# The fourth column pair of the first quarter of both up projections by seven block products instead of eight, with its vector-engine work ordered behind the split of the second half of x

## The chip, the cores and the metric

The kernel runs on one core of a Trainium2 chip. The metric is device time in microseconds (us), lower is better: 1263.74 us is the median of three runs before the change (1261.43 to 1265.73). A core has a matrix engine (TensorE, PE in the profile), a vector engine (VectorE, DVE), a scalar engine (ScalarE, ACT), a general engine (GpSimd, POOL), a queue that here only issues transfers (SyncE, SP), and 16 DMA engines. Each engine runs its instructions in the order in which the program lists them; across engines they wait for each other by semaphores.

## The reference

The program is a trunk of two layers over 512 frames of 1024 features, in float32. Layer 0 mixes by a gated linear recurrence, layer 1 by differential attention over a shared key and value projection. Each layer ends with the same MLP, and each part has a norm before it and one after it. What the change touches is the first product of both MLPs:

```python
D_MODEL = 1024; SEQ = 512; D_FF = 4 * D_MODEL

def squared_relu_mlp(h, w_up, w_down):
    u = jax.nn.relu(h @ w_up)
    return (u * u) @ w_down

# in reference(), per layer
ff = squared_relu_mlp(rms_norm(h, mlp_norm_pre[layer]), mlp_w_up[layer], mlp_w_down[layer])
h = h + rms_norm(ff, mlp_norm_post[layer])
```

`w_up` is 1024 x 4096 and `w_down` 4096 x 1024. The kernel keeps activations transposed: features lie on the 128 partitions, frames along the free axis.

## The kernel before

**Split numbers.** TensorE multiplies a reduced float32 (`fp32r` in the profile). To keep the precision of float32, each operand is split in two, `hi` (a rounded copy, written by ACT) and `lo` (the rest, `value - hi`, written by DVE), and every product is three matmuls (`mm3`, line 114 in the profile through the wrapper `pe.matmul`): hi x hi, hi x lo, lo x hi. Weights come from memory into a `raw` tile (four buffers of 128 x 1024 numbers), ACT writes `whi` from it and DVE writes `wlo` (eight buffers each; `split_w`, lines 172 and 173, `split_b`, lines 200 and 201).

**The MLP.** `block` runs it in four quarters `q` of the 4096 inner columns. In each quarter the up projection makes 1024 inner columns, which are squared and split into `uhi` and `ulo` (`split_u` and `keep_u`, lines 469 to 475), and then the down projection (`dn`) adds their product to `zacc`. An up quarter is four pairs of 256 columns. In quarter 0 all four pairs are computed directly: for each half of the 512 frames and each 128 columns, eight row blocks `kt` of x, three matmuls each, every one 256 frames wide. In quarters 1 to 3 (`up_pairs`, class `Pair`) each pair is a 2 x 2 block product by Strassen's scheme in Winograd's form, with seven products instead of eight: the row blocks of x by even and odd `kt` and by half of the frames make four blocks, and so do the weights. A product is four row blocks of three matmuls, 12 in all. For this a pair needs four weight tiles: "a" (two blocks as they are), "d" (the fourth block; one load for two pairs), "s" and "t" (sums of blocks). The sums of "s" begin in the transfer: SP loads one block twice into the raw tile (line 518) and POOL issues a transfer that adds two others to it (line 519). Those of "t" are made by DVE in the raw tile of "a" (lines 527, 528) before it is split a second time.

**The sums of x.** `sums_x` makes four sums of the blocks of x in place in `zacc` (lines 486 and 488) and splits them: three into tiles `t` of their own (491, 492), the fourth into the place of x's even row blocks of the second half (496, 497), when the direct products have read it. Before the change this stands behind the direct products of quarter 0, and quarter 1 is its first user.

**The order of the work.** PE runs in the order of the program text as `Plan` interleaves it: the main chain (projections) and side chains such as `bounds` (the norms), which are given time by a written estimate of each matmul's cost; `until(("x", name, h))` lets the direct products of half `h` begin when the chain has listed the splits of x's half `h`. The order of ACT, DVE, POOL and SP is made by the framework's scheduler from priorities and its own estimates of when things are ready; side chains have a higher priority. `tc.issue_after(ins)` orders the instructions of its block that stand on the engine of `ins` behind `ins`; it does nothing to other engines. `bounds` for x's second half starts with the last columns of the projection before: sums of squares, a sum over the partitions on PE (`ps_mr`), `rsqrt_rows` (lines 289 to 303, ACT and DVE), then for each of four row block pairs the scaling, the sum with the residual, and x's split: `xhi` on ACT (389), `xlo` on DVE (390), and the store of the residual by POOL (391). The variable `marks` is a dictionary in which instructions are kept for such orderings.

## Time and profile before

| | us |
|---|---|
| median of three runs | 1263.74 |
| lowest and highest | 1261.43, 1265.73 |
| the profiled execution, its own time | 1259.98 |
| its span (first to last instruction) | 1258.1 |
| PE busy in the span | 1234.5 |
| DVE, ACT, POOL busy | 828.9, 669.9, 96.0 |
| mean granted TensorE clock | 0.997 |

Times in profile lines are microseconds from the start of the span. A line of the timeline has the start, the duration, the engine, the line of the kernel, the operation, output and inputs with their shapes and, in brackets, how long the engine had been idle before and what it waited for. A busy PE is not a PE at its peak, since matmuls overlap: the distance between the starts of two matmuls is what counts. Names of tiles stand without their numbers, so `whi_a` is the rounded copy of any "a" tile.

### The profile page before, as it was taken

The page shows a single profiled execution, that of the slowest core. Times are in us where ns is not written, and L with a number is a line of the kernel's source. Part 1 is how long each engine was busy: PE and PEld are TensorE (multiplying, and loading weights), DVE is VectorE, ACT ScalarE, POOL GpSimd, SP SyncE. Part 2 cuts the span into 40 slices and gives each one's busy share as a digit, 9 for nine tenths or more (in the row PEclk, how much of TensorE's full clock was granted, in tenths as well). Part 3 has the DMA queues.
Part 4 walks back from the last instruction along what each step waited for, and adds up shares of the span by engine and source line. Part 5 has one row for each costly group of instructions (what it writes and reads, how often), then busy time and mean ns, then how long its engine had stood idle before and what let it go on. Part 6 is the DMA issues. An engine that isn't in the chain of part 4 may idle for free.

```text
span 1258.1 us, 21436 instructions
## 1 busy us (share of the span) xinstructions
PE 1234.5 (98%) x8440; PEld 1119.2 (89%) x8440; DVE 828.9 (66%) x1649; ACT 669.9 (53%) x1244; POOL 96.0 (8%) x174
## 2 busy tenths in 40 slices
PE   9999999999999999999999999999999999999996
PEld 7889899999988989989999788889998898988996
DVE  6878887867854735636498978564785473663645
ACT  6454545437742724616456877664773371561732
POOL 0202211110000000000100000001000000000000
PEclk9999999999999999999999999999999999999998
DMA  7224544244366564635526322222435365463522
GB/s 255 90 51 116 112 109 122 88 152 137 105 160 130 169 142 109 182 86 145 191 78 192 115 88 84 85 81 88 152 111 150 93 180 120 114 188 77 162 98 67
DMA packets 56726, 156.44 MB, mean 124 GB/s; under 512 B 6289, under 2 KB 8594, under 8 KB 56626
## 3 DMA queue, kind: packets, MB, share of 16 engines
q1 hardware_dynamic: 45920, 120.34, 30.4%
q0 software_dynamic: 10464, 34.61, 13.0%
q8 instruction: 66, 1.08, 0.3%
q14 instruction: 34, 0.28, 0.1%
q10 hardware_dynamic: 242, 0.13, 0.0%
HBM read 145.35 MB, written 9.70 MB: 123 GB/s over the span
## 4 chain that ended last, share of the span: by engine, by line
PE 87%; DVE 5%; ACT 3%; DMA 3%; issue 2%; POOL 0%; SPq 0%; DVEq 0%; ACTq 0%
PE dn L114 21%; PE ux L114 9%; PE up L114 7%; PE qf L114 7%; PE kq L114 6%; PE dn_h L114 5%; PE uz L114 4%; PE bo_h L114 3%; PE ao_h L114 3%; PE gl L114 3%; PE v L114 2%; PE g L114 2%; PE uy L114 2%; PE i L114 2%; PE lg L114 2%
## 5 line engine op out<-in xcount | busy, mean ns | idle before, releaser
L114 PE MATMUL dn<-uhi,whi_dn 128*128 128x512 f32 x384 | 152.0, 396 | 0.0
L114 PE MATMUL dn<-uhi,wlo_dn 128*128 128x512 f32 x384 | 151.9, 396 | 0.0
L114 PE MATMUL dn<-ulo,whi_dn 128*128 128x512 f32 x384 | 151.8, 395 | 0.0
L114 PEld LDWEIGHTS dn<-uhi,whi_dn 128*128 128x128 f32 x384 | 72.2, 188 | 17.8 <-ACT r L570 0.7
L200 ACT ACTIVATE whi_a<-raw_a 128x1024 fp32r<-128x1024 f32 x24 | 25.4, 1058 | 117.5 <-PE dn L114 114.0
L114 PEld LDWEIGHTS dn<-uhi,wlo_dn 128*128 128x128 f32 x384 | 72.2, 188 | 17.4
L114 PEld LDWEIGHTS dn<-ulo,whi_dn 128*128 128x128 f32 x384 | 72.2, 188 | 16.8
L173 DVE TENSOR_TENSOR wlo_dn<-raw_dn,whi_dn 128x1024 fp32r<-128x1024 f32 x64 | 76.6, 1220 | 5.9 <-ACT whi_dn L172 4.6
L475 DVE TENSOR_TENSOR ulo<-r,uhi 128x1024 fp32r<-128x1024 f32 (+1 forms) x40 | 40.2, 1010 | 53.9 <-ACT uhi L474 53.9
L114 PE MATMUL up<-xhi,wlo_up 128*128 128x256 f32 x256 | 72.1, 281 | 1.0 <-DVE wlo_up L173 1.0
L114 PE MATMUL up<-xhi,whi_up 128*128 128x256 f32 x256 | 72.6, 284 | 0.0
L114 PE MATMUL up<-xlo,whi_up 128*128 128x256 f32 x256 | 71.8, 281 | 0.0
L172 ACT ACTIVATE whi_dn<-raw_dn 128x1024 fp32r<-128x1024 f32 x64 | 65.7, 1051 | 7.2 <-PE up L114 3.0
L114 PE MATMUL dn_h<-uhi,whi_dn 128*128 128x256 f32 x240 | 66.6, 278 | 0.0
L114 PE MATMUL dn_h<-uhi,wlo_dn 128*128 128x256 f32 x240 | 66.3, 276 | 0.0
L114 PE MATMUL dn_h<-ulo,whi_dn 128*128 128x256 f32 x240 | 66.3, 276 | 0.0
L617 DVE TENSOR_TENSOR zacc<-dn,zacc 128x512 f32<-128x512 f32 x32 | 22.1, 691 | 59.1 <-PE dn L114 59.0
L519 POOL DMA_DIRECT2D raw_s<-in_w_us_dram x24 | 20.8, 866 | 488.8 <-DMA raw_s<-in_w_us_dram 301.6
L114 PE MATMUL qf<-xhi,whi_qf 128*128 128x512 f32 x128 | 52.7, 411 | 1.2 <-ACT xhi L686 0.6
L200 ACT ACTIVATE whi_t<-raw_a 128x1024 fp32r<-128x1024 f32 x24 | 25.5, 1061 | 49.4 <-PE dn L114 27.2
L114 PE MATMUL qf<-xlo,whi_qf 128*128 128x512 f32 x128 | 50.7, 396 | 0.3 <-DVE xlo L687 0.3
L114 PE MATMUL qf<-xhi,wlo_qf 128*128 128x512 f32 x128 | 50.7, 396 | 0.0
(533 smaller groups left out, 4124.5 us busy)
## 6 DMA issues: line engine op xcount, KB each, us to landing
raw_dn<-in_w_dn_dram SPq DMA_DIRECT2D x64, 512.0 KB, 4.3
raw_a<-in_w_us_dram SPq DMA_DIRECT2D x24, 512.0 KB, 4.3
raw_s<-in_w_us_dram SPq DMA_DIRECT2D x48, 256.0 KB, 4.3
raw_s<-in_w_us_dram POOLq DMA_DIRECT2D x24, 512.0 KB, 6.4
raw_up<-in_w_up_dram SPq DMA_DIRECT2D x16, 512.0 KB, 4.1
raw_wkv<-in_w_kv_dram SPq DMA_DIRECT2D x16, 512.0 KB, 3.7
raw_qf<-in_w_qf_dram SPq DMA_DIRECT2D x14, 512.0 KB, 4.7
raw_d<-in_w_us_dram SPq DMA_DIRECT2D x12, 512.0 KB, 4.4
```

The costliest lines, as they stand in the source:

```text
L114: nc.tensor.matmul(out, lhsT, rhs, **kw)
L172: last_split[:] = [a.activation(hi, raw, AF.Copy)]
L173: v.tensor_tensor(lo, raw, hi.bitcast(F32), op=ALU.subtract)
L200: a.activation(hi, raw, AF.Copy)
L475: v.tensor_tensor(ulo[pr][:, :, lo:hi], r, uhi[pr][:, :, lo:hi].bitcast(F32), op=ALU.subtract)
L519: g.dma_start(rs, ws[p, :, 0:2, :], accum_op=ALU.add)
L617: v.tensor_tensor(z, pss[n4], z, op=ALU.add)
```

## The change

In quarter 0 of both MLPs the first three pairs stay direct. The fourth is computed as a `Pair`, so `sums_x` is now used in quarter 0. The weights are laid out anew for this: `w_up` holds the first 512 columns (four raw tiles) and `w_up2` the next 256 (two raw tiles of four row blocks each); `w_us` holds thirteen pairs in a row in place of three quarters of four. The pair of quarter 0 has a "d" tile of half the size for itself, the later pairs share theirs by twos as before. While this pair's weights are fetched and split, the DVE instructions are ordered behind the last subtraction of x's split (`marks["x"]`, the one of the second half by then).

```diff
@@ -387,7 +387,7 @@
             x = r if gpre is None else t
             a.activation(xhs[pr], x, AF.Copy)
-            v.tensor_tensor(xls[pr], x, xhs[pr].bitcast(F32), op=ALU.subtract)
+            marks["x"] = v.tensor_tensor(xls[pr], x, xhs[pr].bitcast(F32), op=ALU.subtract)
             g.dma_start(res[h][:, 2 * pr:2 * pr + 2, :], r)
...
             def __init__(self, q, p, ts):
-                self.p, self.nm, ws = p, f"{layer}_{q}_{p}", w_us[layer, q - 1]
+                self.p, self.nm = p, f"{layer}_{q}_{p}"
+                n = 4 * q + p - 3
+                ws = w_us[layer, n]
                 self.t1, self.t3, self.t2, self.t4 = ts
...
                 ra = raw("a")
-                nc.sync.dma_start(ra, ws[p, :, 0:3:2, :])
+                nc.sync.dma_start(ra, ws[:, 0:3:2, :])
 
                 rs = raw("s")
                 for i in range(2):
-                    nc.sync.dma_start(rs[:, i, :], ws[p, :, 3, :])
-                g.dma_start(rs, ws[p, :, 0:2, :], accum_op=ALU.add)
-                if p % 2 == 0:
+                    nc.sync.dma_start(rs[:, i, :], ws[:, 3, :])
+                g.dma_start(rs, ws[:, 0:2, :], accum_op=ALU.add)
+                if q == 0:
+                    rd = wp.tile([P, 1, 512], F32, tag="raw", name=f"raw_d{self.nm}", bufs=4)
+                    nc.sync.dma_start(rd, ws[:, 1:2, :])
+                    a22s[:] = split_b(rd, f"d{self.nm}") * 2
+                elif p % 2 == 0:
                     rd = raw("d")
-                    nc.sync.dma_start(rd, ws[p:p + 2, :, 1, :].rearrange("a p f -> p a f"))
+                    nc.sync.dma_start(rd, w_us[layer, n:n + 2, :, 1, :].rearrange("a p f -> p a f"))
                     a22s[:] = split_b(rd, f"d{self.nm}")
...
-        def up_pairs(q, ts):
-
-            one = Pair(q, 0, ts)
+        def up_pairs(q, ts, first=0, after=None):
+
+            with tc.issue_after(after.ins) if after is not None else nullcontext():
+                one = Pair(q, first, ts)
             yield from one.begin()
-            for p in range(1, 5):
+            for p in range(first + 1, 5):
                 yield from one.go_on(p == 4)
                 if p < 4:
                     other = Pair(q, p, ts)
                     yield from other.begin()
                 yield from one.end()
-                one = other
+                if p < 4:
+                    one = other
 
         for q in range(4):
             if q == 0:
-                wt = [load_w(w_up[layer, i], 512, None, f"up{layer}_{i}") for i in range(2)]
+                wt = [load_w(w_up[layer], 512, None, f"up{layer}_0"), load_w(w_up2[layer], 256, None, f"up{layer}_1")]
                 for h, (lo, hi) in enumerate(halves):
                     yield until(("x", name, h))
-                    for pr in range(4):
+                    for pr in range(3):
                         ps = mmt(f"up{layer}_{h}_{pr}").rearrange("p (j t) -> p j t", j=2)
                         for j in range(2):
-                            n = 2 * pr + j
                             for kt in range(8):
-                                wmm(ps[:, j, :], wt[n // 4], kt, (n % 4) * P, xhi, xlo, lo, hi, kt == 0, kt == 7)
+                                wmm(ps[:, j, :], wt[pr // 2], kt, (pr % 2 * 2 + j) * P, xhi, xlo, lo, hi, kt == 0, kt == 7)
                                 yield 0
                         split_u(ps, pr, lo, hi, f"r{layer}_{h}_{pr}")
                 ts = sums_x()
+                yield from up_pairs(q, ts, 3, marks["x"])
             else:
                 yield from up_pairs(q, ts)
```

## The prediction

> **What bounds the kernel now.** I began with the page's first part.

> ```profile
> span 1258.1 us, 21436 instructions
> ...
> PE 1234.5 (98%) x8440; PEld 1119.2 (89%) x8440; DVE 828.9 (66%) x1649; ACT 669.9 (53%) x1244; POOL 96.0 (8%) x174
> ```

> TensorE (PE) is busy 98% of the span, so every matmul taken out shortens the end, unless PE then waits for something that had time to spare. The question is therefore local: how many PE microseconds go, and which of the inputs of the new pair, and of what stands before it, come too late. Next I read where up's first quarter lies in PE's timeline (layer 0; layer 1 runs the same code) and what four pairs by seven products take in the second quarter.

> ```profile
> 304.81 0.28 PE L114 MATMUL up<-xhi,whi_up 128*128 128x256 f32 x1
> ...
> 305.15 0.28 PE L114 MATMUL up<-xhi,whi_up 128*128 128x256 f32 x1
> ...
> 307.77 0.39 PE L114 MATMUL up<-xhi,wlo_up 128*128 128x256 f32 x1 [0.50 <-DVE wlo_up L173]
> ...
> 309.70 1.03 PE L114 MATMUL ps_mr<-ss_ao,onesd 128*128 128x256 f32 x4
> 310.38 0.47 PE L114 MATMUL up<-xhi,whi_up 128*128 128x256 f32 x1
> ...
> 327.52 0.60 PE L114 MATMUL ps_mr<-ss_ao,onesd 128*128 128x256 f32 x2
> 327.77 0.47 PE L114 MATMUL up<-xhi,whi_up 128*128 128x256 f32 x1
> ...
> 351.98 0.39 PE L114 MATMUL dn<-uhi,whi_dn 128*128 128x512 f32 x1
> 352.21 0.39 PE L114 MATMUL dn<-ulo,whi_dn 128*128 128x512 f32 x1
> ...
> 398.45 0.28 PE L114 MATMUL ux<-xhi,whi_a 128*128 128x256 f32 x1
> ...
> 438.62 0.39 PE L114 MATMUL dn<-uhi,whi_dn 128*128 128x512 f32 x1
> ```

> The direct quarter runs from 304.81 to 351.98: 47.17 us for 384 matmuls. Out of that come the wait of 0.50 and the two sums that cut in (309.70 to 310.38 is 0.68, 327.52 to 327.77 is 0.25): 45.74 us, or 0.119 per matmul. There is hardly a wait in it, so PE sets the time here.

> The third view is ACT and DVE around the start of that quarter, because they make x's second half.

> ```profile
> 308.24 1.06 ACT L172 ACTIVATE whi_up<-raw_up 128x1024 fp32r<-128x1024 f32 x1
> 310.92 1.06 ACT L172 ACTIVATE whi_up<-raw_up 128x1024 fp32r<-128x1024 f32 x1 [1.61 <-DMA raw_up<-in_w_up_dram]
> 312.33 1.06 ACT L172 ACTIVATE whi_up<-raw_up 128x1024 fp32r<-128x1024 f32 x1 [0.35 <-DMA raw_up<-in_w_up_dram]
> 313.29 0.46 ACT L289 ACTIVATE ss_ao<-ps_mr,epsc 128x256 f32<-128x256 f32 x1
> 313.78 0.42 ACT L297 ACTIVATE ss_ao<-ss_ao 128x256 f32<-128x256 f32 x1
> ```

> ```profile
> 306.49 1.22 DVE L173 TENSOR_TENSOR wlo_up<-raw_up,whi_up 128x1024 fp32r<-128x1024 f32 x1
> ...
> 307.96 1.22 DVE L173 TENSOR_TENSOR wlo_up<-raw_up,whi_up 128x1024 fp32r<-128x1024 f32 x1
> ...
> 314.56 0.42 DVE L299 SCALAR_TENSOR_TENSOR ss_ao<-ps_mr,ss_ao 128x256 f32<-128x256 f32 x1
> ...
> 325.73 0.68 DVE L390 TENSOR_TENSOR xlo<-zacc,xhi 128x512 fp32r<-128x512 f32 x1
> 326.33 0.42 DVE L341 TENSOR_TENSOR ss_ao<-ss_ao 128x256 f32<-128x256 f32 x1
> 326.67 2.48 DVE L486 TENSOR_TENSOR zacc<-zacc 128x1024 f32<-128x1024 f32 x2
> ...
> 337.19 0.69 DVE L475 TENSOR_TENSOR ulo<-r,uhi 128x512 fp32r<-128x512 f32 x1 [0.56 <-ACT uhi L474]
> ...
> 348.49 0.69 DVE L475 TENSOR_TENSOR ulo<-r,uhi 128x512 fp32r<-128x512 f32 x1 [3.52 <-ACT uhi L474]
> ```

> The reader is to see a queue that holds up the x chain. The sum that L289 reads is done at 309.70 + 1.03 = 310.73, yet L289 starts at 313.29, because two weight copies whose transfers land late stand before it on ACT. From L299 on the chain is dense; the last split of x's second half (L390) ends at 325.73 + 0.68 = 326.41. PE wants that half after 192 matmuls, at 304.81 + 192 x 0.119 + 0.50 + 0.68 + 0.25 = 329.1. So the late copies cost nothing today: x is 2.7 us early.

> **The change part by part.**

> *Removed on PE.* A pair computed directly is 96 matmuls, 96 x 0.119 = 11.43 us. By seven products it is 84. The four pairs of the second quarter took 438.62 - 398.45 = 40.17, or 10.04 each; the waits in them were

> ```profile
> PE ux L114 <- DVE r L565: 0.5, 1, 0.5
> ```

> so 9.92 without. The gain is 1.39 to 1.51 per MLP; I take 1.45, so 2.9 us for both. The floor is 12 matmuls at the spacing by which the quarter starts (304.81 to 305.15 for three, 0.113), 1.36. [...]

> *Moved: the need for x's second half.* The first half now has 144 matmuls and ends at 304.81 + 144 x 0.119 + 0.50 + 0.68 = 323.1. Its last two of eight row blocks of x are wanted 18 matmuls into the second half, at 323.1 + 2.1 = 325.2. If the chain stayed where it is, PE would wait 326.4 - 325.2 = 1.2 us. But the two late copies of up weights go: six up tiles are left, the last copied at 308.24. What takes their place on ACT is the pair's own copies (a and d), which the new ordering on the x split doesn't hold, since that split and the queueing are DVE's. The transfers take, from issue to landing (last column, us):

> ```profile
> raw_s<-in_w_us_dram SPq DMA_DIRECT2D x48, 256.0 KB, 4.3
> raw_s<-in_w_us_dram POOLq DMA_DIRECT2D x24, 512.0 KB, 6.4
> ```

> There are four raw buffers. Block "a" takes the buffer and the time of the old seventh up tile, so its copy could run at 310.92 and end at 311.98. "s" takes that of the fourth, free at 306.49 + 1.22 = 307.7. "d" comes third, in the buffer free at 307.96 + 1.22 = 309.2, and lands 4.3 later at 313.5. Bounds: no copy ahead of L289, L289 at 310.8, x 2.5 us earlier, no wait; both ahead, a half-size copy (0.62 for 512 columns, estimated from half of 1.06 and some overhead) at 313.5 ends at 314.1, L299 at about 315.0, x at 326.9 and a wait of 1.7. Between: "a" alone ahead, L289 at 312.0, x at 325.1, wait 0. I take the middle, since "a" stands exactly where the seventh tile stood, and "d" one buffer later than the eighth.

> *Added: weights of the pair, per MLP.* From the second quarter:

> ```profile
> 395.31 1.22 DVE L201 TENSOR_TENSOR wlo_a<-raw_a,whi_a 128x1024 fp32r<-128x1024 f32 x1 [1.56 <-ACT whi_a L200]
> 396.57 0.69 DVE L527 TENSOR_TENSOR raw_a<-raw_a,raw_s 128x512 f32<-128x512 f32 x1
> ...
> 398.31 0.68 DVE L528 TENSOR_TENSOR raw_a<-raw_a 128x512 f32<-128x512 f32 x1
> ...
> 400.21 1.23 DVE L201 TENSOR_TENSOR wlo_t<-raw_a,whi_t 128x1024 fp32r<-128x1024 f32 x1 [0.61 <-ACT whi_t L200]
> ```

> Back to back on DVE a 1.22 us subtract takes 1.14 and a 0.69 one 0.60. So d 0.6, a 1.14, s 1.14, the two sums 1.2, t 1.14: 5.2 us of DVE, and 0.6 + 3 x 1.06 = 3.8 on ACT. Two up splits (2.3 and 2.1) and one u split go. Cover: the 17.4 us of direct matmuls of the second half. These end at 323.1 + 144 x 0.119 + 0.25 = 340.5; a is wanted then, s one product (1.43) later at 341.9, t at 343.4, the fourth x sum at 349.1.

> *Moved: the sums of x.* They were covered by the quarter's rest and dn; now they are wanted at 341.9 and 343.4. DVE's block from 326.33 to 337.19 + 0.69 = 337.88 holds them, 0.56 idle and four u splits, one of which goes: 10.4 us. With x 1.3 earlier it starts at 325.0 and ends at 335.4. Then d, a, s, the two sums and one u split: 4.1 + 0.6, to 340.1. Copy t on ACT until 341.3, its subtract until 342.5: 0.9 before its need. It holds only if copy t isn't behind the last direct pair's relu, square and copy and the fourth sum's copies, which come due at 340.5:

> ```profile
> 352.55 0.57 ACT L469 ACTIVATE r<-up 128x512 f32<-128x512 f32 x1
> 353.02 0.41 ACT L496 ACTIVATE xhi<-zacc 128x256 fp32r<-128x256 f32 x1
> 353.33 0.62 ACT L473 ACTIVATE r<-r 128x512 f32<-128x512 f32 x1
> ...
> 354.80 0.62 ACT L474 ACTIVATE uhi<-r 128x512 fp32r<-128x512 f32 x1
> ```

> These four take 1.9 back to back; behind them, t is ready at about 344.7 and PE waits 1.3. The first product's eviction, on the same bank as the third, would have the same delay. So 0 to 2 us per MLP; I take 0.7.

> *Costed at nothing.* Buffers for s and t come free with up's first two tiles, 78 matmuls into the second half, 323.1 + 9.3 = 332.4, eight before their need. The accumulating transfer of s stands on POOL with the four stores of the residual, the last of which is

> ```profile
> 323.70 0.54 POOL L391 DMA_DIRECT2D res_ao<-rs_ao  x1 [1.66 <-DVE rs_ao L380]
> ```

> Even behind it, s has landed at 324.2 + 0.9 + 6.4 = 331.5, under the buffer's 332.4; without that cover it would hold t by the same amount. dn's tiles: only the first finds a raw buffer early, the next waits until "a" is done at 342.5, lands at 347 and is split by 349.5; dn starts at 350.5 and takes its second tile 24 matmuls of 0.23 later, at 356. Cover 6 us.

> *Sum.* Per MLP -1.45 + 0 + 0.7 = -0.75; both: -1.5. The profiled execution took 1259.98 (span 1258.1 and 1.9 around it), so 1258.5 for it. The runs shown have a median of 1263.74, 3.8 above it; there -1.5 gives 1262.2.

> **The rivals.**

> *All of it hidden* (0.25): no copy before L289, t in time: -2.9, 1260.8. For it: DVE has 0.9 to spare by the sum above. Against it: the copies of up's seventh and eighth tile did stand before L289.

> *x late* (0.20): a and d both before L289, 1.7 of wait for x: per MLP -1.45 + 1.7 + 0.7 = +0.95, both +1.9, 1265.6. For it: that is the order of the eighth tile today. Against it: d's buffer comes 1.5 us later than the eighth tile's predecessor's.

> *Slower* (0.15): the pair's weights late on DVE. With x at 326.9, both u splits (1.2), dn's first tile (1.14) and the four lows of the fourth sum (1.5) queued before the t subtract, DVE is through at 326.9 + 10.4 + 4.1 + 3.8 = 345.2, t at 347.6, wanted at 342.2 + 2.9 = 345.1: 2.5 us of wait besides x's 1.7, per MLP +2.75, both +5.5, 1269.2. It decides once the waits exceed 3.35 per MLP (2.9 + 3.8 in both). For it: DVE was without a gap from 314.6 to 337; against it: the gap of 3.52 us at the end of this quarter before, where a u split waits for ACT, shows that DVE's load then falls off.

> **How the numbers follow.** The forecast has 0.40, the rivals 0.25, 0.20 and 0.15. I take 0.3% (3.8 us) as what can be told from no change. Forecast and x-late lie within it; all-hidden is 0.9 from the bound, so a third of it and a little of the forecast may show as faster: 0.15, with something for a gain not seen here 0.17. Slower holds the last rival and a little of x-late: 0.18. Same has the rest, 0.65. The range leaves out the slow rival's far end and goes 2 us below all-hidden for the runs' own spread (1261.43 to 1265.73): 1259.0 to 1268.0.

> **What would show it.** 24 matmuls fewer than 8440, but for records that a trace misses; the direct part ending near 340.5 and dn starting near 350 in layer 0. L289 before 312.5 confirms the x step; after 313.5 refutes it. A wait of up for xlo or xhi at the start of the second half shows x late; waits of ux for wlo_t, whi_t or the first eviction show the weights late. A wait of dn for wlo_dn, or one of uz for the accumulating transfer, would be a cost I put at nothing, and any PE wait over 3 us makes the forecast wrong.

## The result and the profile after

The changed kernel takes 1273.08 us (median of four runs, 1272.42 to 1274.39) against 1262.73 for the kernel before in the same comparison (four runs, 1261.43 to 1265.73): a ratio of 1.008, 95% interval 1.0059 to 1.0101. It is slower, by 10.4 us, and above the forecast range (1259.0 to 1268.0). The profiled execution of the changed kernel took 1273.44 us.

The page of the changed kernel, first part:

```profile
span 1271.4 us, 21414 instructions
...
PE 1237.5 (97%) x8416; PEld 1120.6 (88%) x8416; DVE 836.4 (66%) x1661; ACT 675.0 (53%) x1252; POOL 98.0 (8%) x176
```

The 24 matmuls are gone (8440 to 8416), yet PE is busy 3.0 us longer and the span grew by 13.3. Where that happened is read from the first quarter of up in each MLP, from its first up matmul to the first matmul of dn. Stretches of the kernel before, layer 0 and layer 1 (start:end, length, then busy us of PE, PEld, DVE, ACT and POOL with their instructions, granted clock, DMA share, GB/s):

```profile
304.81:351.98 47.17, 46.67 (x392) 46.32 (x391) 37.81 (x52) 36.23 (x62) 2.16 (x4) 1.00 0.43 146
900.44:947.62 47.18, 46.66 (x393) 46.31 (x392) 37.73 (x52) 36.50 (x63) 2.16 (x4) 1.00 0.44 147
```

The same two stretches of the changed kernel:

```profile
305.68:359.03 53.35, 48.31 (x381) 47.21 (x379) 43.74 (x63) 39.00 (x67) 3.09 (x5) 0.94 0.48 147
907.59:960.24 52.65, 47.87 (x380) 46.76 (x379) 43.70 (x63) 39.56 (x69) 3.08 (x5) 0.97 0.50 147
```

The two quarters grew by 6.18 and 5.47, together 11.65 of the 13.3; the other 1.65 lies outside them (0.87 before the first quarter, 0.10 between the two, 0.68 behind the second). PE's idle time, length less busy, went from 0.50 and 0.52 to 5.04 and 4.78. And PE's busy time went up by 1.64 and 1.21 although 12 matmuls left each quarter, with a granted clock of 0.94 and 0.97 where it had been 1.00. So there are two losses, waits and clock (the granted clock is the share of full speed that the profile records for PE). The waits of PE in the changed kernel (total, times, longest):

```profile
PE ux L114 <- ACT p L546: 6.5, 2, 3.6
PE up L114 <- DVE xlo L390: 2.3, 4, 0.7
...
PE up L114 <- DVE wlo_up L173: 1.0, 2, 0.5
```

The last row was there before. The other two are new (the row left out belongs to other quarters: in layer 0's and layer 1's first quarter these three are all that is listed).

**The first new wait: x's second half.** ACT in the changed kernel, layer 0:

```profile
311.64 0.48 ACT L289 ACTIVATE ss_ao<-ps_mr,epsc 128x256 f32<-128x256 f32 x1 [1.04 <-PE ps_mr L114]
312.15 0.42 ACT L297 ACTIVATE ss_ao<-ss_ao 128x256 f32<-128x256 f32 x1
316.18 0.63 ACT L200 ACTIVATE whi_d<-raw_d 128x512 fp32r<-128x512 f32 x1 [3.61 <-DMA raw_d<-in_w_us_dram]
316.71 1.04 ACT L200 ACTIVATE whi_a<-raw_a 128x1024 fp32r<-128x1024 f32 x1
...
319.48 0.89 ACT L387 ACTIVATE zacc<-rs_ao,gn 128x256 f32<-128x256 f32 x2
```

L289 starts early, at 311.64. But the copies of d and a stand two instructions further on, behind L297 and ahead of L387, which is in the middle of the chain that makes x. ACT stands still for 3.61 us until d has landed. The transfer was issued by SP at 310.08 and took about 6 us; the DMA issues of the changed kernel (count, size, median us from issue to landing):

```profile
raw_d<-in_w_us_dram SPq DMA_DIRECT2D x2, 256.0 KB, 6.5
```

DVE waits behind that, and its last split of x ends at 327.27 + 0.68 = 327.95:

```profile
321.44 0.69 DVE L390 TENSOR_TENSOR xlo<-zacc,xhi 128x512 fp32r<-128x512 f32 x1 [3.40 <-ACT xhi L389]
...
327.27 0.68 DVE L390 TENSOR_TENSOR xlo<-zacc,xhi 128x512 fp32r<-128x512 f32 x1
...
341.55 0.69 DVE L534 TENSOR_TENSOR raw_a<-raw_a 128x512 f32<-128x512 f32 x1
...
343.38 1.23 DVE L201 TENSOR_TENSOR wlo_t<-raw_a,whi_t 128x1024 fp32r<-128x1024 f32 x1 [0.53 <-ACT whi_t L200]
```

By itself this costs PE 2.3 us in both MLPs together. It also moves everything that DVE does for the pair: the sum that t is copied from is ready only at 341.55 + 0.69 = 342.24.

**The second new wait: the first eviction.** ACT in the changed kernel from the copy of t on:

```profile
342.28 1.06 ACT L200 ACTIVATE whi_t<-raw_a 128x1024 fp32r<-128x1024 f32 x1 [2.74 <-DVE raw_a L534]
343.25 1.04 ACT L172 ACTIVATE whi_dn<-raw_dn 128x1024 fp32r<-128x1024 f32 x1
344.19 0.70 ACT L496 ACTIVATE xhi<-zacc 128x256 fp32r<-128x256 f32 x2
344.81 1.05 ACT L172 ACTIVATE whi_dn<-raw_dn 128x1024 fp32r<-128x1024 f32 x1
...
347.37 1.04 ACT L172 ACTIVATE whi_dn<-raw_dn 128x1024 fp32r<-128x1024 f32 x1
348.31 0.62 ACT L474 ACTIVATE uhi<-r 128x512 fp32r<-128x512 f32 x1
348.83 0.36 ACT L546 ACTIVATE p<-ux 128x256 f32<-128x256 f32 x1
```

The eviction of the pair's first product (L546, its copy out of the bank in which PE adds it up) is the last of a row without a gap: the late copy of t, three copies of dn's weights, the four copies of the fourth x sum, and the last direct pair's relu, square and copy. The third product uses the first one's bank, so PE waits. In PE's timeline:

```profile
342.74 0.28 PE L114 MATMUL ux<-xhi,whi_a 128*128 128x256 f32 x1
...
345.40 0.28 PE L114 MATMUL uz<-t,wlo_s 128*128 128x256 f32 x1
349.25 0.80 PE L114 MATMUL ux<-t,whi_t 128*128 128x256 f32 x2 [3.56 <-ACT p L546]
...
351.98 0.41 PE L114 MATMUL uy<-xhi,whi_a 128*128 128x256 f32 x1
352.19 0.41 PE L114 MATMUL uy<-xlo,whi_a 128*128 128x256 f32 x1
...
951.54 0.50 PE L114 MATMUL ux<-t,whi_t 128*128 128x256 f32 x2 [2.98 <-ACT p L546]
```

**The clock.** The matmuls behind that wait stand 0.21 apart (351.98 to 352.19) and not 0.11 to 0.12. Stretches of the changed kernel (columns as above; the third figure from the end is the granted clock):

```profile
348.00:349.00 1.00, 0.00 (x0) 0.00 (x0) 0.77 (x2) 1.00 (x3) 0.00 (x0) 0.71 0.73 291
349.00:350.00 1.00, 0.75 (x3) 0.76 (x4) 1.00 (x2) 1.00 (x3) 0.00 (x0) 0.50 0.96 246
...
354.00:355.00 1.00, 1.00 (x7) 1.00 (x7) 0.22 (x1) 0.44 (x1) 0.00 (x0) 0.50 0.72 295
...
356.00:357.00 1.00, 1.00 (x11) 1.00 (x11) 1.00 (x2) 0.63 (x1) 0.00 (x0) 1.00 0.00 0
```

In layer 0 the clock falls to half during the wait and comes back only some 6 us after PE has resumed: about 28 matmuls at 0.213 where 0.117 was usual, 28 x 0.096 = 2.7 us. In layer 1 it is at 0.50 from about 952.5 to 956.0, so it falls 1 us after PE has resumed at 951.54: some 17 matmuls, 1.6 us.

### The profile page after: what moved, and what is told of

The parts are those of the page before. It is cut to its first block, busy times and chain, and to the rows that moved or that the text cites. A ratio compares the mean times of both kernels' runs of the same rounds, so it can differ in the third digit from the quotient of the medians.

```text
span 1271.4 us, 21414 instructions
## 1 busy us (share of the span) xinstructions
PE 1237.5 (97%) x8416; PEld 1120.6 (88%) x8416; DVE 836.4 (66%) x1661; ACT 675.0 (53%) x1252; POOL 98.0 (8%) x176
## 3 DMA queue, kind: packets, MB, share of 16 engines
q8 instruction: 66, 1.08, 0.4%
## 4 chain that ended last, share of the span: by engine, by line
PE 75%; DVE 8%; DMA 7%; ACT 6%; issue 3%; POOL 0%; SPq 0%; DVEq 0%; ACTq 0%; POOLq 0%
PE dn L114 20%; PE ux L114 7%; PE qf L114 6%; PE kq L114 6%; PE dn_h L114 5%; DMA raw_s<-in_w_us_dram 4%; PE bo_h L114 3%; PE ao_h L114 3%; PE uz L114 3%; PE gl L114 3%; PE v L114 2%; PE g L114 2%; PE i L114 2%; PE lg L114 2%; DMA raw_d<-in_w_us_dram 2%
## 5 line engine op out<-in xcount | busy, mean ns | idle before, releaser
L114 PE MATMUL dn<-uhi,whi_dn 128*128 128x512 f32 x384 | 151.9, 396 | 0.0
L114 PE MATMUL dn<-ulo,whi_dn 128*128 128x512 f32 x384 | 151.9, 396 | 0.0
L114 PE MATMUL dn<-uhi,wlo_dn 128*128 128x512 f32 x384 | 151.9, 395 | 0.0
L200 ACT ACTIVATE whi_a<-raw_a 128x1024 fp32r<-128x1024 f32 x26 | 27.5, 1058 | 122.0 <-PE dn L114 117.9
L114 PEld LDWEIGHTS dn<-uhi,whi_dn 128*128 128x128 f32 x384 | 72.2, 188 | 17.8 <-ACT r L576 0.7
L114 PEld LDWEIGHTS dn<-uhi,wlo_dn 128*128 128x128 f32 x384 | 72.2, 188 | 17.3
L114 PEld LDWEIGHTS dn<-ulo,whi_dn 128*128 128x128 f32 x384 | 72.2, 188 | 16.9
L173 DVE TENSOR_TENSOR wlo_dn<-raw_dn,whi_dn 128x1024 fp32r<-128x1024 f32 x64 | 77.1, 1220 | 3.8 <-ACT whi_dn L172 3.6
L475 DVE TENSOR_TENSOR ulo<-r,uhi 128x1024 fp32r<-128x1024 f32 (+1 forms) x38 | 40.1, 1054 | 48.0 <-ACT uhi L474 48.0
L172 ACT ACTIVATE whi_dn<-raw_dn 128x1024 fp32r<-128x1024 f32 x64 | 66.1, 1052 | 9.2 <-PE ux L114 4.0
L114 PE MATMUL dn_h<-uhi,whi_dn 128*128 128x256 f32 x240 | 66.6, 278 | 0.0
L114 PE MATMUL dn_h<-uhi,wlo_dn 128*128 128x256 f32 x240 | 66.3, 276 | 0.0
L114 PE MATMUL dn_h<-ulo,whi_dn 128*128 128x256 f32 x240 | 66.3, 276 | 0.0
L200 ACT ACTIVATE whi_t<-raw_a 128x1024 fp32r<-128x1024 f32 x26 | 27.6, 1061 | 54.6 <-DVE raw_a L534 27.4
L114 PE MATMUL up<-xlo,whi_up 128*128 128x256 f32 x192 | 54.1, 282 | 2.3 <-DVE xlo L390 2.3
L114 PE MATMUL up<-xhi,wlo_up 128*128 128x256 f32 x192 | 53.9, 281 | 1.0 <-DVE wlo_up L173 1.0
L114 PE MATMUL up<-xhi,whi_up 128*128 128x256 f32 x192 | 54.7, 285 | 0.0
L114 PE MATMUL qf<-xhi,whi_qf 128*128 128x512 f32 x128 | 53.0, 414 | 1.1 <-ACT xhi L694 0.8
L200 ACT ACTIVATE whi_s<-raw_s 128x1024 fp32r<-128x1024 f32 x26 | 27.6, 1060 | 45.9 <-PE dn L114 30.9
L114 PE MATMUL qf<-xlo,whi_qf 128*128 128x512 f32 x128 | 50.7, 396 | 0.3 <-DVE xlo L695 0.3
## 6 DMA issues: line engine op xcount, KB each, us to landing
raw_dn<-in_w_dn_dram SPq DMA_DIRECT2D x64, 512.0 KB, 4.1
raw_a<-in_w_us_dram SPq DMA_DIRECT2D x26, 512.0 KB, 4.6
raw_s<-in_w_us_dram SPq DMA_DIRECT2D x52, 256.0 KB, 4.4
raw_s<-in_w_us_dram POOLq DMA_DIRECT2D x26, 512.0 KB, 6.2
raw_wkv<-in_w_kv_dram SPq DMA_DIRECT2D x16, 512.0 KB, 3.7
raw_qf<-in_w_qf_dram SPq DMA_DIRECT2D x14, 512.0 KB, 4.8
raw_up<-in_w_up_dram SPq DMA_DIRECT2D x12, 512.0 KB, 4.1
raw_d<-in_w_us_dram SPq DMA_DIRECT2D x12, 512.0 KB, 3.8
```

Source lines behind the costliest of these rows:

```text
L114: nc.tensor.matmul(out, lhsT, rhs, **kw)
L172: last_split[:] = [a.activation(hi, raw, AF.Copy)]
L173: v.tensor_tensor(lo, raw, hi.bitcast(F32), op=ALU.subtract)
L200: a.activation(hi, raw, AF.Copy)
L475: v.tensor_tensor(ulo[pr][:, :, lo:hi], r, uhi[pr][:, :, lo:hi].bitcast(F32), op=ALU.subtract)
```

## The experiments

My theory after the result: the loss is a late ACT queue (d and a inside the x chain, dn's copies ahead of the eviction) whose wait of about 3 us also halves the clock. The rivals: the clock has another cause; one of the two orders alone explains it; the change's order on DVE is to blame. e1 to e4 were timed beside one set of runs of the kernel before (median 1262.63, 21 runs), e6 to e9 beside another (1262.27, 14 runs).

| kernel | median us | ratio to before, 95% | quarter, layer 0 (idle) | quarter, layer 1 (idle) |
|---|---|---|---|---|
| before | 1262.63, 1262.27 | | 47.17 (0.50) | 47.18 (0.52) |
| after | 1273.08 | 1.008 (1.0059 to 1.0101) | 53.35 (5.04) | 52.65 (4.78) |
| e1_fill | 1270.21 | 1.0056 (1.0043 to 1.007) | 50.34 (1.45) | 51.30 (2.71) |
| e2_xact | 1262.39 | 0.9999 (0.9989 to 1.0008) | 47.32 (1.70) | 47.25 (1.72) |
| e3_dnlate | 1264.58 | 1.0011 (0.9999 to 1.0024) | 47.27 (1.82) | 48.31 (2.73) |
| e4_both | 1257.93 | 0.9961 (0.9948 to 0.9973) | 44.90 (0.51) | 46.02 (0.52) |
| e6_nodve | 1267.80 | 1.0044 (1.003 to 1.0058) | 49.57 (2.07) | 50.58 (2.36) |
| e7_hold8 | 1268.57 | 1.0051 (1.0036 to 1.0067) | 50.11 (3.13) | 47.83 (3.49) |
| e8_hold16 | 1277.31 | 1.0117 (1.0102 to 1.0132) | 53.48 (6.46) | 52.84 (5.96) |
| e9_actonly | 1259.45 | 0.9981 (0.9971 to 0.999) | 46.01 (0.51) | 45.36 (0.00) |

**e1_fill: is the clock a cost of its own?** The changed kernel, with twelve matmuls that nobody reads in the place of PE's wait:

```diff
                 self.p, self.nm = p, f"{layer}_{q}_{p}"
+                self.first = q == 0
...
             def go_on(self, alone):
+                if self.first:
+                    dummy = smt(f"fill{self.nm}")
+                    for _ in range(12):
+                        nc.tensor.matmul(dummy[:, 0:P], onesd, onesd, start=True, stop=True)
                 yield from self.prod(self.x, self.s2, self.t2, False)
```

> The changed kernel with 12 matmuls on constants put on PE in front of the third product of the new pair in both MLPs (about 2.6 us of work nobody reads), inside the wait of about 3.7 us (layer 0) and 3.0 us (layer 1) that PE has there. Theory (the wait itself, and then a halved clock that the wait brings on, 0.50 granted for some 6 us in layer 0 and 3.5 us in layer 1): the idle stretch shrinks to about 1 us, the clock stays at 1.00 and the time falls by about 4.6 us, from 1273.1 to about 1268.5, although work is added. Rival (the clock falls for another reason, as the load of the other engines): the halved stretches stay, the time is 1273 or more.

Measured: 1270.21. The profile shows the added work (it lists each of the twelve twice) and what is left of the wait (PE's timeline):

```profile
345.37 2.84 PE L560 MATMUL fill<-onesd 128*128 128x128 f32 x24
348.51 0.51 PE L114 MATMUL ux<-t,whi_t 128*128 128x256 f32 x2 [0.30 <-ACT p L547]
```

The eviction is nearly as late as before (348.09 where it was 348.83), but the granted clock stays at 1.00 in both quarters, where it was 0.94 and 0.97, and the kernel is about 3 us faster than the changed one (by the ratios 1.008 - 1.0056 = 0.0024 of 1262.7) with 2.84 us more of PE work in each MLP. So the clock is a cost of its own, and PE's standing still is what brought it about here. The forecast was 1.7 too low: layer 1 gained only 1.35 and still waited 0.9 for the eviction and 1.3 for x.

**e2_xact: the pair's ACT copies behind the x chain.** The instructions of the pair's construction are ordered behind the last `xhi` copy on ACT as well as behind the last `xlo` split on DVE:

```diff
-            a.activation(xhs[pr], x, AF.Copy)
+            marks["xa"] = a.activation(xhs[pr], x, AF.Copy)
...
-            with tc.issue_after(after.ins) if after is not None else nullcontext():
+            with ExitStack() as st:
+                for m in after or ():
+                    st.enter_context(tc.issue_after(m.ins))
                 one = Pair(q, first, ts)
...
-                yield from up_pairs(q, ts, 3, marks["x"])
+                yield from up_pairs(q, ts, 3, (marks["x"], marks["xa"]))
```

> The changed kernel with the new pair's ACT instructions ordered behind the last xhi copy too, so that copies d and a no longer stand in the middle of the chain that makes x's second half. Theory: L387 no longer waits for the transfer of d, x's second half comes some 3 us earlier, PE's waits for xlo (2.3 us in both MLPs) go; the sums of x and the weights come earlier too, so the wait for the first eviction shrinks but stays, since dn's copies still stand before it: 1264 to 1268. Rival (the order of d and a costs only the 2.3 us): 1270.8, with the wait for the eviction and the halved clock as they were.

Measured: 1262.39, better than expected and 10.2 us under the changed kernel by the ratios. Stretches of e2:

```profile
305.60:352.92 47.32, 45.62 (x381) 45.03 (x379) 43.66 (x63) 39.33 (x68) 3.09 (x5) 1.00 0.53 165
902.08:949.33 47.25, 45.53 (x381) 44.95 (x379) 43.61 (x63) 39.54 (x69) 3.08 (x5) 1.00 0.55 165
```

No wait for x is left. With x earlier, the copy of t starts at 338.71 and not 342.28. The three dn copies still stand ahead of the eviction, but the wait for it is 1.2 in each MLP and the clock stays at 1.00. These rows also give a yardstick for the changed kernel's busy time: the same matmuls at full clock take 45.62 and 45.53, so the clock cost it 48.31 - 45.62 = 2.7 and 47.87 - 45.53 = 2.3 (of the latter the 17 slow matmuls explain 1.6; the spacing also differs between executions, from 330.6 to 333.5 it is 0.118 in before and 0.114 in the changed kernel).

**e3_dnlate: dn's first weight tiles behind the eviction.** The changed kernel, with the copies of dn's first four weight tiles of quarter 0 ordered on ACT behind the second product's eviction (DVE's half follows by its data):

```diff
-                a.activation(t, ps, AF.Copy)
+                marks[name] = a.activation(t, ps, AF.Copy)
                 return t
...
-                    wt = load_w(w_dn[layer, q, i], 512, None, f"dn{layer}_{q}_{i}")
+                    with tc.issue_after(marks["p5"].ins) if (q, i) == (0, 0) else nullcontext():
+                        wt = load_w(w_dn[layer, q, i], 512, None, f"dn{layer}_{q}_{i}")
```

> The changed kernel with the split of dn's first four weight tiles of quarter 0 ordered on ACT and DVE (ACT: behind the eviction of the new pair's second product). Theory (three dn copies of 1.05 us before the first eviction are what makes its wait long): the wait falls from 3.6 and 3.0 us to under 1 us each, the clock stays at 1.00, x's waits of 2.3 us stay: about 1273.1 - 6 - 4.6 = 1262.5. Rival (the eviction is late because the t copy and the last direct pair's work are late, so that taking the dn copies away moves little): 1270 or more, clock still halved.

Measured: 1264.58, 2 above the expectation and far from the rival. ACT in e3:

```profile
316.74 0.63 ACT L200 ACTIVATE whi_d<-raw_d 128x512 fp32r<-128x512 f32 x1 [3.43 <-DMA raw_d<-in_w_us_dram]
...
342.84 1.06 ACT L200 ACTIVATE whi_t<-raw_a 128x1024 fp32r<-128x1024 f32 x1 [2.73 <-DVE raw_a L534]
...
346.84 0.37 ACT L546 ACTIVATE p<-ux 128x256 f32<-128x256 f32 x1
...
347.37 2.00 ACT L172 ACTIVATE whi_dn<-raw_dn 128x1024 fp32r<-128x1024 f32 x2
```

The copy of t is as late as ever, and x too. From the copy of t to the eviction it is now 4.0 us, where it was 6.55. PE waits 1.0 in each MLP for the eviction, and the clock stays at 1.00.

**e4_both: e2 and e3 together.**

> Both orderings together. Theory (those two orders of ACT are the whole of the loss): the 24 matmuls saved remain, about 1260 to 1261, 1.5 to 3 us under the kernel before, with no PE wait over 0.7 us in quarter 0. Rival (something else in the change costs, as the new layout of the weights or the 24 further transfers): 1264 or more though the waits are gone.

Measured: 1257.93 (five runs, 1257.79 to 1259.88), better than expected, and 0.27 to 0.52% faster than the kernel before: a version that beats both. Stretches of e4:

```profile
304.81:349.71 44.90, 44.39 (x380) 43.93 (x379) 41.10 (x60) 37.34 (x66) 3.08 (x5) 1.00 0.49 148
899.41:945.43 46.02, 45.50 (x381) 45.04 (x380) 41.09 (x60) 37.98 (x67) 3.08 (x5) 1.00 0.49 143
```

Only the old wait of 0.5 for up's first weights remains. The quarters are 2.27 and 1.16 shorter than before, the spans 2.4 (1258.1 to 1255.7); against the median of before it is 4.7, because the profiled execution of before was a quick one. Of the 2.27 in layer 0, 1.1 is not the change but a narrower spacing of the matmuls in that quarter (last section). The parts do not add up: by the ratios e2 alone takes 10.2 us off the changed kernel, e3 alone 8.7, both 15.0. Each alone brings the wait down to about 1 us (1.2 and 1.0), where the clock stayed at 1.00, so each earns the clock once.

**e6_nodve: the order on DVE taken out.** The changed kernel without its new ordering (`up_pairs(q, ts, 3)` with no instruction to stand behind):

```diff
-                yield from up_pairs(q, ts, 3, marks["x"])
+                yield from up_pairs(q, ts, 3)
```

> The changed kernel without its ordering on DVE, and with none on ACT: copies d and a stand in the chain on ACT as in the changed kernel, and their splits stand in it on DVE as well. Theory (the x chain is what hurts): another 1 to 2 us of wait for xlo per MLP, and the wait for the eviction with its halved clock stays: 1274 to 1278. Rival (the pair's weights come earlier and so t and the eviction too, which outweighs x): under 1271.

Measured: 1267.80. My expectation fell and the rival held: without its ordering the change is 4.5 us less slow (1.008 - 1.0044). DVE in e6:

```profile
316.92 0.69 DVE L201 TENSOR_TENSOR wlo_d<-raw_d,whi_d 128x512 fp32r<-128x512 f32 x1 [3.28 <-ACT whi_d L200]
317.87 1.23 DVE L201 TENSOR_TENSOR wlo_a<-raw_a,whi_a 128x1024 fp32r<-128x1024 f32 x1
...
328.81 0.68 DVE L390 TENSOR_TENSOR xlo<-zacc,xhi 128x512 fp32r<-128x512 f32 x1
...
334.96 0.68 DVE L534 TENSOR_TENSOR raw_a<-raw_a 128x512 f32<-128x512 f32 x1
```

The splits of d and a now stand in the x chain on DVE, and x is done at 329.49, 1.5 later than in the changed kernel; but the sum behind t is ready at 335.64 and not at 342.24, and no wait for the eviction is listed. PE waits for x instead, three times in each MLP. Waits and stretches of e6:

```profile
PE up L114 <- DVE xlo L390: 4.2, 6, 0.8
```

```profile
326.42:329.83 3.41, 2.02 (x13) 1.46 (x12) 3.41 (x8) 3.41 (x8) 0.54 (x1) 1.00 0.20 77
329.83:333.25 3.42, 3.42 (x18) 3.42 (x18) 3.42 (x5) 2.62 (x5) 0.00 (x0) 0.50 0.01 2
```

Here no single wait is over 0.8 us, but from 326.42 to 329.83 PE is busy for only 2.02 of 3.41 us, and the clock halves all the same.

**e9_actonly: the DVE order taken out of e4.** e4 with the order behind `marks["xa"]` only:

```diff
-                yield from up_pairs(q, ts, 3, (marks["x"], marks["xa"]))
+                yield from up_pairs(q, ts, 3, (marks["xa"],))
```

> Both orderings of ACT, but without the change's own ordering on DVE (behind the last xlo). Theory (DVE's splits of d and a follow their copies, and these stand behind the x split on ACT, so that the ordering on DVE is idle): as with both, about 1258. Rival (DVE's ordering does something of its own): over 1260.

Measured: 1259.45, between expectation and rival. Once ACT's copies stand behind the x chain, DVE's halves follow by their data, and waits and clock are those of e4. The 1.5 us between the medians (2.5 by the ratios, whose intervals just overlap) are not in the two quarters, which add up to 91.37 in e9 and 90.92 in e4; an effect of the DVE order beside the ACT order is neither shown nor excluded.

**e7_hold8 and e8_hold16 (8 and 16 copies): how long a wait halves the clock?** e4, with 8 or 16 copies of the first product on ACT ahead of its eviction; nobody reads them:

```diff
                 yield from self.prod(self.x, self.a11, xpart(0, 0), True)
+                if self.first:
+                    for _ in range(8):
+                        hold = pool.tile([P, 256], F32, tag="hold", name=f"hold{self.nm}{_}", bufs=1)
+                        a.activation(hold, self.x, AF.Copy)
                 self.p1 = self.keep(self.x, "p1")
```

> The kernel with both orderings, and in front of the new pair's first eviction eight further copies of the same product on ACT (0.26 us each, nobody reads them), in both MLPs, so that PE waits for the eviction: some 1.5 us per MLP. Theory (a wait below some 3 us costs itself and no more): the clock stays at 1.00, the time is 1257.9 + 2 x 1.5, about 1261. Rival (any wait at this place brings the halved clock): 1264 or more, with clock 0.50 after the wait.

> The same with sixteen copies: a wait of some 3.6 us per MLP. Theory (a wait near 3 us or longer brings a halved clock for 3.5 to 6 us besides, worth 1.7 to 2.9 us of PE): clock 0.50 behind the wait in at least one of the MLPs, 1257.9 + 2 x 3.6 + 2 x 2.3, about 1269.7. Rival (the clock has nothing to do with the wait): clock 1.00 throughout, about 1265.1.

Measured: 1268.57 and 1277.31. The copies took 0.41 us each (eight take 3.28, sixteen 6.61), more than I had counted, so e7's waits came out at 2.63 and 2.98 where I wanted 1.5, and e8's at 6.0 in each MLP. e7 therefore doesn't test a short wait, though its time is on the rival's side (1264 or more); e2 and e3 do, with 1.0 to 1.2 and no drop. With the waits as measured, e8's sum would be 1257.9 + 2 x 6.0 + 2 x 2.3 = 1274.5; the other 2.8 are not accounted for. What e7 does show is that here the length of a wait alone did not decide. Stretches of e7, in layer 0 and then in layer 1:

```profile
344.03:347.45 3.42, 0.79 (x7) 0.59 (x6) 0.24 (x1) 3.23 (x10) 0.00 (x0) 1.00 0.00 1
347.45:350.86 3.41, 3.41 (x18) 3.41 (x18) 2.36 (x2) 2.86 (x4) 0.00 (x0) 0.50 0.17 26
```

```profile
941.37:944.78 3.41, 1.53 (x14) 1.33 (x12) 1.26 (x3) 3.19 (x9) 0.00 (x0) 1.00 0.50 154
944.78:948.19 3.41, 2.31 (x19) 2.31 (x20) 1.10 (x1) 3.38 (x8) 0.00 (x0) 1.00 0.00 0
948.19:951.61 3.42, 3.42 (x32) 3.42 (x32) 3.42 (x6) 2.30 (x4) 0.00 (x0) 1.00 0.65 196
```

The wait of 2.63 in layer 0 halved the clock, the longer one of 2.98 in layer 1 of the same execution did not (while 2.98 in layer 1 of the changed kernel did). The stretches are 3.41 us long, counted on from the fall of the clock at 347.45 (last section): the first wait lies in one stretch and leaves PE 0.79 us of work in it; the second is split between two, with 1.53 and 2.31. The drop came without transfers: in the first of these stretches the DMA share is 0.00. e7's quarters show the price: PE busy 46.98 in layer 0, 44.34 in layer 1. e8's waits of 6.0 halved it both times.

## Why the prediction was wrong, step by step

- **Removed on PE** (1.45 per MLP): right in kind, a little large. At full clock the quarter's busy time fell by 1.05 and 1.13 (e2), 1.22 and 1.08 (e3), 2.28 and 1.16 (e4), 1.17 and 1.30 (e9), 1.30 in the mean, under my floor of 1.36 in seven of eight; the eighth, 2.28, owes 1.1 to a narrower spacing (0.113 and not 0.118, last section), and the seven others have a mean of 1.16. Why twelve matmuls fewer save less than twelve spacings (12 x 0.117 = 1.40) stays open.
- **Moved: the need for x's second half** (0 taken, 1.7 at most): the step that failed first. I asked only whether the copies of d and a would stand ahead of L289. My own sign, L289 before 312.5, came true (311.64), and x was late nevertheless, because the copies stood behind L297 and held L387. A queue can be cut at any instruction of the chain, and I priced one place. The landing was mis-sized as well: 310.08 + 6.1 = 316.18 for d where I had 313.5, with 4.3 for the transfer from a median of other moments. The wait for x, 2.3 in both MLPs, is in the range of my bound; that a, s, both sums and t slide with it by some 3 us was not carried on.
- **Added weights and moved sums** (0.7 taken, 0 to 2): t itself was in time (343.38 + 1.23 = 344.61, wanted when PE began to wait, at 349.25 - 3.56 = 345.69), so the wait for it that I priced did not come. I had said that the first eviction "would have the same delay" as t behind 1.9 us of ACT work. It had that delay plus three dn copies of 0.96 and the late start: 3.56 and 2.98.
- **Costed at nothing, dn's tiles**: I looked at when dn needs them, not at what they hold up. dn's own start had cover; the copies' place on ACT, ahead of the eviction, had none. I also had the tiles come too late for that, the second landing at 347: the buffers of d and s were free for the second and third, issued at 335.85 and 341.59, and their copies ran at 344.81 and 347.37, before the eviction at 348.83. e3 shows the price: 8.7 us, the clock included.
- **The missing term**: the sum had no clock. I wrote that any wait over 3 us would make the forecast wrong, but gave such a wait only its own length. With the waits came another 2.7 and 2.3 us. Layer 0 closes with it: 46.67 to 45.62 is -1.05, idle +4.54, clock +2.69, together +6.18.
- **The rivals**: the slower one had the right sign and partly the right place (the pair's weights late behind x on DVE), but stopped at 1269.2 without ACT's queue and the clock. "All of it hidden" (1260.8) is nearest to what e4, with two orderings more, makes of the change (1257.93).
- **Direct part and dn**: 340.5 and 350 were forecast, 342.74 and 359.03 measured (0.87 of it from the later start).

## What to carry to other kernels

When a change adds transfers and copies to an engine's queue, list every instruction of the chain that others wait for on that engine and ask at each whether a late copy can stand ahead of it; work "with time to spare" must be checked for what it stands in front of. An ordering on one engine does not hold the halves of the same helper on another. And where PE would stand still for about as long as it did here (one wait of 2.63 us or more, or several short ones that left it 2.02 busy of 3.41), a half clock is to be priced beside the wait, here at 1.6 to 2.7 us; one wait of 2.98 (e7, layer 1) cost only itself.
